# A decoder layer with product-key experts: three blocks of token tiles (2, 4, 2) in place of two (5, 3)

## The chip, the core and the metric

The kernel runs on one NeuronCore of a Trainium2 chip. The metric is the device time of one launch in microseconds. Before the change the median of three runs is 3268.28 us (3263.65 to 3278.97). TensorE multiplies matrices, VectorE and ScalarE work on rows of 128 partitions, GpSimd does row work too and issues the indirect transfers (gathers); SyncE issues most other transfers. Each engine runs its own list of instructions in order and waits at semaphores.

## The reference, cut to what matters

The layer has 1024 tokens of 1024 columns, in float32. Cut to its steps:

```
mod = silu(c) @ ada_w + ada_b                     # six vectors: sh1, sc1, g1, sh2, sc2, g2
h   = rms_norm(x) * (1 + sc1) + sh1
proj = h @ w_in                                   # latents of attention A, queries, keys, values of attention B
A: 4 heads, q and k/v from low-rank latents, rotary part of 64 columns, causal softmax
B: 4 heads, two softmax maps, (p1 - lambda * p2) @ v, norm of each head
x   = x + g1 * (concat(A, B) @ w_out)
h2  = rms_norm(x) * (1 + sc2) + sh2
q   = h2 @ w_q                                    # 8 heads, 2 halves of 128 columns
s   = q . sub_keys (128 keys for each half); top 16 of each half; top 16 of the 256 sums
g   = softmax of the 16 sums; e = their experts (first key * 128 + second key)
y   = sum over the 128 chosen experts of  g * gelu(u_tab[e] . h2) * v_tab[e]
out = x + g2 * y
```

`u_tab` and `v_tab` have 16384 rows of 1024 columns (64 MB each).

## The kernel before, in words

A tile is 128 tokens, so there are eight, 0 to 7. The products of the float32 operands are made in three passes over a high and a low part (`split`, `passes`, lines 272 to 286): weights come in raw, ScalarE writes the high part and VectorE or GpSimd the low part. The line numbers in profiles name these helpers often: 274 is the high part, 275 the low part, 284 to 286 the three passes.

The trunk has these stages. `project` (line 289) makes queries, keys and values of all eight tiles, with each weight loaded and split once, and puts them into DRAM. `block(t0, n)` (line 1200) then takes n tiles through `attend` (scores, softmax, values), `output` (output projection, residual, second norm) and `queries` (queries against keys, lists of the 16 best). It runs once for tiles 0 to 4 and once for tiles 5 to 7. In the second one the low parts of the weights are made on GpSimd, and `route_dense` (line 859) runs beside it: for each of the tiles 0 to 4 `routing` finds the chosen pairs on VectorE, and `matrix` makes, token by token, two one-hot rows A and B whose outer product on TensorE (line 897, tile `pg`) gives the token's weights over 128 x 128 experts. The rows B are made by GpSimd (line 886), by ScalarE or by VectorE after the letters of `SHARE`. The weights go to DRAM (`gd`).

The experts (line 1011) take tiles 0 to 4, 640 tokens, through all 16384 experts. Step j of 128 loads 128 rows of `u`, splits them, multiplies them with the tokens (`mm_u`, tile `mm`, line 1072), takes the Gelu, multiplies with the weights (`weigh`), splits the result, and adds products with rows of `v` four steps later (`mm_v`, tiles `pj` and `tp`, three passes; `add_y`).

Tiles 5 to 7 go another way beside it (`gathered`, line 929): for each of the 128 choices a gather brings the 128 chosen rows of `u` (512 KB, line 948 on GpSimd), and VectorE takes the dot product with the token (line 973). Then the same with rows of `v`: four gathers are one group, whose product with a window of coefficients goes to `y` on TensorE (line 993). The buffers of the gathers (`gath`, seven) turn in order; a gather waits for the one who read its buffer last. `PACE` says how far `gathered` is let on in each step of the experts.

The order of instructions in the trunk comes from a scheduler that follows the order of tracing and its own timeline; `weave` traces several streams in step by their costs. In the experts the order is the traced one (`manual_schedule`). PSUM has eight banks, which each stage takes by `banks`.

## Time and profile before

| | |
|---|---|
| median of 3 runs | 3268.28 us (3263.65 to 3278.97) |
| span of the profiled execution | 3271.8 us |
| TensorE busy | 3063.6 us, 94% |
| VectorE busy | 2180.9 us, 67% |
| ScalarE busy | 1199.3 us, 37% |
| GpSimd busy | 1288.8 us, 39% |
| read and written in HBM | 707.74 MB and 83.38 MB |
| mean granted TensorE clock | 0.974 |

The profiled execution's span is 3.5 us above the median and inside the range of the runs. Busy time is the time in which at least one instruction of the engine ran. In rows, PE is TensorE (PEld its weight loads), DVE VectorE, ACT ScalarE, POOL GpSimd, SP SyncE. A name such as `mm<-h2d,uh` says what is written and what is read. The stages of the trunk can be told by time: projections to 376 us, attention of tiles 0 to 4 to 505, their output to 584, their queries to 718, the second block and the matrices to 1189, and then the experts.

### The profile page before, as it was taken

What the parts mean: (1) busy time and instruction counts of PE and PEld (TensorE: products, weight loads), DVE (VectorE), ACT (ScalarE), POOL (GpSimd) and SP (SyncE); (2) the same over time, 40 slices, a digit from 0 to 9 for tenths busy, and PEclk for the clock granted to TensorE, in tenths of its full rate; (3) what the DMA queues carried; (4) which work ended last, traced back from release to release, by engine and by line L of the source; (5) the groups of instructions that cost most, each with busy time, mean ns of one, the idle gap of its engine ahead of it and who ended that gap; (6) DMA issues with size and microseconds to landing.
All of it is one profiled execution on the core that took longest, in us unless ns stands there. A gap on an engine that the chain in (4) does not pass through costs nothing.

```text
span 3271.8 us, 49470 instructions
## 1 busy us (share of the span) xinstructions
PE 3063.6 (94%) x17865; PEld 2569.6 (79%) x17865; DVE 2180.9 (67%) x5138; ACT 1199.3 (37%) x2372; POOL 1288.8 (39%) x1197
## 2 busy tenths in 40 slices
PE   6999989988887977999999999999999999999998
PEld 3678777977776967998888888888787888887776
DVE  4767366799898987888876666655665665633334
ACT  4644383337778862223222222222222222222221
POOL 1120000004799734334444444544454545523440
PEclk9999999989898999999999999999999999999999
DMA  8653637513357655778888888888888988878884
GB/s 268 200 167 113 206 99 240 182 36 120 116 178 238 182 155 198 267 257 285 300 281 295 289 296 302 305 317 312 310 306 316 322 323 318 310 271 292 285 295 158
DMA packets 375572, 794.38 MB, mean 243 GB/s; under 512 B 31392, under 2 KB 171040, under 8 KB 368672
## 3 DMA queue, kind: packets, MB, share of 16 engines
q0 software_dynamic: 114544, 418.46, 36.5%
q1 hardware_dynamic: 153200, 311.16, 28.1%
q10 hardware_dynamic: 107584, 61.61, 6.4%
q8 instruction: 140, 2.29, 0.3%
q14 instruction: 104, 0.85, 0.1%
HBM read 707.74 MB, written 83.38 MB: 242 GB/s over the span
## 4 chain that ended last, share of the span: by engine, by line
PE 66%; DVE 9%; DMA 8%; issue 6%; ACT 4%; POOL 3%; SPq 0%; POOLq 0%; ACTq 0%; DVEq 0%
PE mm L1072 20%; PE pj L284 6%; PE pj L285 6%; PE pj L286 6%; PE y L993 5%; PE tp L284 3%; PE tp L285 3%; PE tp L286 3%; PE pg L897 3%; DMA gath<-in_peer_v,eT 2%; DMA vr<-in_peer_v 2%; POOL gath L948 2%; DVE gath L973 1%; PE ov L655 1%; POOL B L886 1%
## 5 line engine op out<-in xcount | busy, mean ns | idle before, releaser
L1072 PE MATMUL mm<-h2d,uh 128*128 128x320 f32 x4096 | 774.3, 311 | 4.8 <-ACT C L1079 4.0
L948 POOL DMA_INDIRECT gath<-in_peer_u,ei x384 | 436.1, 1136 | 730.8 <-DVE gath L973 496.8
L1072 PEld LDWEIGHTS mm<-h2d,uh 128*128 128x128 f32 x4096 | 647.3, 189 | 44.6 <-issue 25.2
L948 POOL DMA_INDIRECT gath<-in_peer_v,eT x384 | 436.5, 1137 | 336.1 <-PE y L993 191.4
L973 DVE SCALAR_TENSOR_TENSOR gath<-gath,h 128x1024 f32<-128x1024 f32 x384 | 465.4, 1223 | 91.5 <-DMA gath<-in_peer_u,ei 73.6
L1072 PE MATMUL mm<-h2d,ul 128*128 128x320 f32 x2048 | 469.1, 310 | 20.3 <-POOL ul L275 13.3
L274 ACT ACTIVATE vh<-vr 128x512 fp32r<-128x512 f32 x256 | 160.6, 629 | 691.9 <-DMA vr<-in_peer_v 358.7
L886 POOL TENSOR_SCALAR B<-iota,T 128x128 f32<-128x128 f32 x240 | 264.1, 1108 | 269.7 <-DVE T L871 198.2
L275 DVE TENSOR_TENSOR vl<-vr,vh 128x512 fp32r<-128x512 f32 x248 | 169.8, 691 | 298.4 <-ACT vh L274 232.5
L1072 PEld LDWEIGHTS mm<-h2d,ul 128*128 128x128 f32 x2048 | 343.7, 189 | 22.0 <-POOL ul L275 13.7
L1079 ACT ACTIVATE C<-mm 128x640 f32<-128x640 f32 x128 | 89.6, 700 | 570.4 <-PE mm L1072 490.1
L1083 DVE TENSOR_TENSOR C<-C,G 128x640 f32<-128x640 f32 x128 | 105.2, 822 | 254.3 <-ACT C L1079 215.5
L285 PE MATMUL pj<-vl,CH 128*128 128x512 f32 x640 | 252.3, 394 | 11.1 <-POOL vl L275 9.5
L284 PE MATMUL tp<-vh,CH 128*128 128x512 f32 x640 | 255.4, 399 | 4.8 <-DVE cT L984 2.9
L285 PE MATMUL tp<-vl,CH 128*128 128x512 f32 x640 | 252.3, 394 | 3.1 <-DVE vl L275 2.3
L284 PE MATMUL pj<-vh,CH 128*128 128x512 f32 x640 | 254.6, 398 | 0.5 <-ACT vh L274 0.3
L286 PE MATMUL tp<-vh,CL 128*128 128x512 f32 x640 | 250.5, 391 | 0.0
L286 PE MATMUL pj<-vh,CL 128*128 128x512 f32 x640 | 250.4, 391 | 0.0
L897 PE MATMUL pg<-B,A 128*128 128x128 f32 x1280 | 197.0, 301 | 51.2 <-POOL B L886 21.9
L897 PEld LDWEIGHTS pg<-B,A 128*128 128x128 f32 x1280 | 177.4, 209 | 69.3 <-POOL B L886 35.5
L274 ACT ACTIVATE uh<-ur 128x512 fp32r<-128x512 f32 x256 | 157.9, 621 | 188.9 <-DMA ur<-in_u_t 166.7
L993 PE MATMUL y<-gath,zb 128*32 128x512 f32 x1536 | 202.4, 599 | 6.1 <-DMA gath<-in_peer_v,eT 6.0
(320 smaller groups left out, 5802.3 us busy)
## 6 DMA issues: line engine op xcount, KB each, us to landing
ur<-in_u_t SPq DMA_DIRECT2D x256, 256.0 KB
vr<-in_peer_v SPq DMA_DIRECT2D x256, 256.0 KB
gd<-gs ACTq DMA_DIRECT2D x20, 2048.0 KB
G<-gd SPq DMA_DIRECT2D x31, 1280.0 KB
adaw<-in_ada_w SPq DMA_DIRECT2D x32, 512.0 KB
wraw<-in_peer_w_q SPq DMA_DIRECT2D x128, 128.0 KB
wraw<-in_w_out SPq DMA_DIRECT2D x32, 256.0 KB
wraw<-in_w_in SPq DMA_DIRECT2D x24, 256.0 KB
```

The costliest lines, as they stand in the source:

```text
L274: nc.scalar.activation(hi, src, AF.Copy)
L275: (eng or nc.vector).tensor_sub(lo, src, hi.bitcast(FT))
L284: nc.tensor.matmul(out, ah, bh, start=start, stop=False)
L285: nc.tensor.matmul(out, ah, bl, start=False, stop=False)
L286: nc.tensor.matmul(out, al, bh, start=False, stop=stop)
L886: nc.gpsimd.tensor_scalar(B[:, m, :], iota128, T[:, 1, c + m:c + m + 1], T[:, 2, c + m:c + m + 1], op0=OP.is_equal, op1=OP.mult)
L897: nc.tensor.matmul(pg[:, o, :], A[:, o, :], B[:, o, :], start=True, stop=True)
L948: nc.gpsimd.indirect_dma_start(out=u, out_offset=None, in_=tab, in_offset=bass.IndirectOffsetOnAxis(ap=idx, axis=0))
L973: nc.vector.scalar_tensor_tensor(got[n], got[n], 1.0, q["h2"], op0=OP.mult, op1=OP.mult, accum_out=q["dots"][:, s:s + 1])
L993: nc.tensor.matmul(q["y"][RB * k:RB * k + RB, c, :], z[:, k, m % 2, RB - 1 - m:2 * RB - 1 - m], got[n + k][:, c * 512:(c + 1) * 512], star ...
L1072: nc.tensor.matmul(ps[:, o, 0:C2], s[:, k % 4, :], h2[:, mv, k, o * C2:(o + 1) * C2], start=st, stop=(k == 7 and s is l))
L1083: nc.vector.tensor_mul(c, c, gt[j // NJ][:, :, j % NJ, :])
```

## The change

The tiles are taken in three blocks: A is tiles 0 and 1, D tiles 2 to 5, B tiles 6 and 7. Block A goes through the whole trunk alone. Then the rest of the trunk (projections of D, block D, projections of B, block B beside `route_dense` for D) is woven with `gathered` for A, which is spread over 700 units of cost by `paced`. The experts take D, 512 tokens, and gather for B. So `project` runs three times and loads and splits its weights each time; `output` and `queries` run three times too, and GpSimd makes their low parts for D and B (`t0` is not 0). The gathers beside the trunk have five buffers (`NGA`), those beside the experts six (`NG`). `y` has its two PSUM banks for the whole run, so other stages have fewer: the projections four, the scores three or two, and `mm_u` now has two single banks (`mu`) in turn, for 512 columns each. The matrices are written for 16 tokens at a time and read by eight steps (`JG`), with two buffers. The shares of the one-hot rows are now half on GpSimd, with more on ScalarE and fewer on VectorE. Comments were taken out, which moves the line numbers: 886 is 882 now, 948 is 945, 973 is 970, 993 is 990, 1072 is 1060.

```diff
-DT = 5
-TOK = DT * P
+A0, AN = 0, 2
+D0, DN = 2, 4
+B0, BN = 6, 2
+TOK = DN * P
...
-GB = 32
+GB = 16
...
-SHARE = ['PAPDPAPD', 'PAPDPAPD', 'PAPDPAPD', 'PDADPDAD', 'DDADPDAD']
+SHARE = ['PAPAPAPD', 'PAPAPAPD', 'PAPAPAPD', 'PAPDPAPD']
...
+    ys = ctx.enter_context(tc.tile_pool(name="ys", bufs=1, space=PSUM, reuse_waits="tile"))
...
-            banks(c1, **(dict(mm=2, ov=1, pg=1) if t0 else dict(sc=4, ov=2)))
+            banks(c1, **(dict(sc=2, ov=1, pg=1) if t0 == B0 else dict(sc=3, ov=1)))
...
-            units = ([(kind, h, i, heads[kind, h]) for h in range(4) for kind in "md" for i in range(n)] if t0 else [(kind, h, i, heads[kind, h]) for h in range(4) for i in range(n) for kind in "md"])
+            units = [(kind, h, i, heads[kind, h]) for h in range(4) for kind in "md" for i in range(n)]
...
-    NG = 7
+    NG = 6
+    NGA = 5
-    def gathered(ts, w, rp, gath, zb):
+    def gathered(ts, w, rp, gath, zb, NG):
...
-            banks(c1, mm=1, ys=1, pj=2)
+            banks(c1, mu=2, pj=2)
...
-                        for o in range(2):
-                            nc.tensor.matmul(ps[:, o, 0:C2], s[:, k % 4, :], h2[:, mv, k, o * C2:(o + 1) * C2],
-                                             start=st, stop=(k == 7 and s is l))
+                        nc.tensor.matmul(ps, s[:, k % 4, :], h2[:, mv, k, :], start=st, stop=(k == 7 and s is l))
...
-            V = (((0, 0), (0, 1)), ((0, 2), (0, 3), (0, 4)), ((1, 0), (1, 1)), ((1, 2), (1, 3), (1, 4)))
+            V = (((0, 0), (0, 1)), ((0, 2), (0, 3)), ((1, 0), (1, 1)), ((1, 2), (1, 3)))
...
+    def projected(t0, n):
+        with ExitStack() as c1:
+            banks(c1, pj=4)
+            yield from project(t0, n)
+
+    def paced(g, total):
+        done = 0.0
+        for f in g:
+            yield (f - done) * total
+            done = f
...
-        run(weave((project(0, NT), 1.0), (ada_rest(), 0.2)))
+        run(weave((project(A0, AN), 1.0), (ada_rest(), 0.3)))
...
-        lists = pool(c1, "lists", DT)
-        run(block(0, DT))
-        run(weave((block(DT, NT - DT), 1.0), (route_dense(range(DT)), 2.6)))
+        gath = pool(c1, "gathA", NGA)
+        run(block(A0, AN))
+        def rest():
+            nonlocal lists
+            yield from projected(D0, DN)
+            lists = pool(c1, "lists", DN)
+            yield from block(D0, DN)
+            yield from projected(B0, BN)
+            yield from weave((block(B0, BN), 1.0), (route_dense(range(D0, D0 + DN), rp), 2.6))
+        run(weave((rest(), 1.0),
+                  (paced(gathered(list(range(A0, A0 + AN)), w, rp, gath, zb, NGA), 700.0), 1.0)))
     trunk.close()
-    experts()
+    experts(w, rp, zb)
```

GpSimd's order while the matrices are made, in the kernel before (B are one-hot rows, wl low parts of query weights; x is how many follow each other):

```order
L886 TENSOR_SCALAR B<-iota_98,T 128x128 x15
L275 TENSOR_TENSOR wl<-wraw,wh 128x256 x2
L886 TENSOR_SCALAR B<-iota_98,T 128x128
L275 TENSOR_TENSOR wl<-wraw,wh 128x256 x2
L886 TENSOR_SCALAR B<-iota_98,T 128x128 x3
L275 TENSOR_TENSOR wl<-wraw,wh 128x256 x2
```

The same place after the change, and GpSimd's way from there into the experts (gath are gathers, G the matrices, ul and vl low parts of the tables):

```order
L945 DMA gath<-in_peer_v,eT 128x1024 x4
L281 TENSOR_TENSOR wl<-wraw,wh 128x256 x2
L882 TENSOR_SCALAR B<-iota_101,T 128x128 x2
L281 TENSOR_TENSOR wl<-wraw,wh 128x256 x2
L882 TENSOR_SCALAR B<-iota_101,T 128x128 x4
L945 DMA gath<-in_peer_v,eT 128x1024 x4
L882 TENSOR_SCALAR B<-iota_101,T 128x128 x10
L945 DMA gath<-in_peer_v,eT 128x1024 x4
L882 TENSOR_SCALAR B<-iota_101,T 128x128 x12
L945 DMA gath<-in_peer_v,eT 128x1024 x59
L1053 DMA G<-gd 128x4096
L281 TENSOR_TENSOR ul<-ur,uh 128x512 x8
```

Gathers of block A now stand between the one-hots and the low parts, and 59 of the 512 stand behind the last one-hot, in front of all that GpSimd does for the experts.

TensorE's order at the same border, before (pg are the matrices, tp key scores, mm the first products of the experts):

```order
L897 MATMUL pg<-B,A 128x128 x8
L775 MATMUL tp<-keys,qh 128x128 x4
L1072 MATMUL mm<-h2d,uh 128x320 x4
L897 MATMUL pg<-B,A 128x128 x8
L775 MATMUL tp<-keys,qh 128x128 x2
L897 MATMUL pg<-B,A 128x128 x24
L1072 MATMUL mm<-h2d,ul 128x320 x2
L1072 MATMUL mm<-h2d,uh 128x320 x4
```

And after it (y are the products of gathered rows, eight to a group of four gathers, mu what mm was):

```order
L1060 MATMUL mu<-h2d,uh 128x512 x2
L893 MATMUL pg<-B,A 128x128 x16
L990 MATMUL y<-gath,zb_1554 32x512
L893 MATMUL pg<-B,A 128x128 x8
L990 MATMUL y<-gath,zb_1554 32x512
L893 MATMUL pg<-B,A 128x128 x4
L990 MATMUL y<-gath,zb_1554 32x512 x13
L990 MATMUL y<-gath,zb_1555 32x512 x16
L990 MATMUL y<-gath,zb_1554 32x512 x16
...
L990 MATMUL y<-gath,zb_1555 32x512 x16
L1060 MATMUL mu<-h2d,ul 128x512
```

After the last `pg` 125 rows of `y` follow each other (one row of 13 and seven of 16), and the experts come behind them.

## Rows read from the trace of the kernel before

**Rows 1.** Windows by stage, busy us: PE, PEld, DVE, ACT, POOL; clock; DMA:

```profile
0.00:45.00 45.00, 14.88 (x76) 3.37 (x76) 9.74 (x36) 9.16 (x17) 13.79 (x32) 0.97 0.91 300
45.00:376.00 331.00, 320.67 (x1656) 251.23 (x1657) 208.26 (x499) 165.56 (x407) 38.63 (x56) 0.98 0.53 165
376.00:505.00 129.00, 107.27 (x724) 91.50 (x723) 78.91 (x235) 92.80 (x248) 0.00 (x0) 0.93 0.54 154
505.00:584.00 79.00, 72.14 (x351) 60.24 (x349) 45.82 (x73) 24.75 (x52) 1.14 (x2) 0.94 0.80 290
584.00:718.00 134.00, 124.17 (x848) 122.51 (x849) 119.04 (x734) 45.30 (x109) 0.00 (x0) 0.95 0.27 82
718.00:882.00 164.00, 137.36 (x940) 120.60 (x940) 151.95 (x423) 119.65 (x232) 82.67 (x76) 0.94 0.42 126
882.00:1050.00 168.00, 134.06 (x767) 118.05 (x767) 144.01 (x330) 126.95 (x236) 154.61 (x135) 0.87 0.59 188
1050.00:1189.00 139.00, 130.77 (x910) 125.38 (x910) 134.84 (x514) 123.03 (x270) 98.46 (x110) 0.98 0.60 171
...
1262.00:3272.00 2010.00, 1975.12 (x11309) 1632.62 (x11307) 1233.55 (x2106) 464.50 (x759) 882.13 (x774) 0.99 0.83 292
```

**Rows 2.** Timeline of PE at the first experts: start, us, what, idle before:

```profile
1189.83 0.83 PE L1072 MATMUL mm<-h2d,uh 128*128 128x320 f32 x4
...
1216.46 0.90 PE L1072 MATMUL mm<-h2d,ul 128*128 128x320 f32 x2 [12.67 <-POOL ul L275]
```

**Rows 3.** Chain in order of time, in the experts: start, us, what:

```profile
1340.50 2.37 DVE gath L973 x4
...
1411.29 7.04 PE mm L1072 x48
1423.79 7.04 PE mm L1072 x48
```

**Rows 4.** Timeline of PE, second table's passes:

```profile
1409.99 0.39 PE L285 MATMUL pj<-vl,CH 128*128 128x512 f32 x1
1410.22 0.39 PE L286 MATMUL pj<-vh,CL 128*128 128x512 f32 x1
```

**Rows 5.** Groups by line: count, then busy us, mean ns, idle before:

```profile
L886 POOL TENSOR_SCALAR B<-iota,T 128x128 f32<-128x128 f32 x240 | 264.1, 1108 | 269.7 <-DVE T L871 198.2 <-PE pg L897 50.4 <-DVE nm L554 3.2
...
L993 PE MATMUL y<-gath,zb 128*32 128x512 f32 x1536 | 202.4, 599 | 6.1 <-DMA gath<-in_peer_v,eT 6.0
...
L275 POOL TENSOR_TENSOR wl<-wraw,wh 128x256 fp32r<-128x256 f32 (+1 forms) x80 | 74.4, 942 | 25.3 <-ACT wh L274 18.1 <-PE pg L897 3.2 <-PE tp L775 1.1
L275 DVE TENSOR_TENSOR wl<-wraw,wh 128x256 fp32r<-128x256 f32 (+3 forms) x120 | 63.2, 540 | 26.0 <-ACT wh L274 24.6 <-DMA wraw<-in_w_out 0.7 <-DMA wraw<-in_peer_w_q 0.5
```

**Rows 6.** Timeline of POOL, the first gathers:

```profile
1262.34 1.03 POOL L948 DMA_INDIRECT gath<-in_peer_u,ei  x1 [5.87 <-DVE ei L852]
1263.68 0.95 POOL L948 DMA_INDIRECT gath<-in_peer_u,ei  x1 [0.31 <-issue]
1264.93 0.94 POOL L948 DMA_INDIRECT gath<-in_peer_u,ei  x1 [0.30 <-issue]
...
1271.69 1.75 POOL L948 DMA_INDIRECT gath<-in_peer_u,ei  x1 [0.85 <-DVE gath L973]
```

**Rows 7.** Line 886: ns shortest, median, longest:

```profile
L886 POOL TENSOR_SCALAR B<-iota,T x240: 781/964/3799, 761.2 to 1199.1; 128x128 f32<-128x128 f32 x120
```

**Rows 8.** Timeline of PE, gathered rows of the last tile:

```profile
3171.45 1.92 PE L993 MATMUL y<-gath,zb 128*32 128x512 f32 x16
...
3177.97 1.90 PE L993 MATMUL y<-gath,zb 128*32 128x512 f32 x10 [0.67 <-DMA gath<-in_peer_v,eT]
```

**Rows 9.** Timeline of POOL, the gather between:

```profile
3173.63 0.94 POOL L948 DMA_INDIRECT gath<-in_peer_v,eT  x1 [6.21 <-PE y L993]
```

**Rows 10.** Timeline of DVE, the first dot products:

```profile
1270.19 1.22 DVE L973 SCALAR_TENSOR_TENSOR gath<-gath,h 128x1024 f32<-128x1024 f32 x1 [8.13 <-DMA gath<-in_peer_u,ei]
...
1276.84 2.29 DVE L973 SCALAR_TENSOR_TENSOR gath<-gath,h 128x1024 f32<-128x1024 f32 x1
```

More of the change, by code (lines that the diff above doesn't have):

```diff
@@ L316, in loadx @@
             def loadx(t):
-                xs[t] = wn.tile([P, D], FT, name="xt")
+                xs[t] = wn.tile([P, D], FT, name="xt", bufs=2 if t0 == A0 else 1)
                 nc.sync.dma_start(xs[t], xin[t])
@@ L565, in scores @@
             def scores(terms, L):
-                if t0:
-                    m = mmt()
-                    ps = [(m, 0, L)]
-                else:
-                    ps = [(bank("sc"), c, min(c + 512, L)) for c in range(0, L, 512)]
+                ps = [(bank("sc"), c, min(c + 512, L)) for c in range(0, L, 512)]
                 for b, c0, e0 in ps:
@@ L581, in turned @@
             def turned(w, L):
-                pT = pp.tile([P, nk, P], FT, name="pT", bufs=2 if t0 else 3)
+                pT = pp.tile([P, nk, P], FT, name="pT", bufs=2 if t0 == B0 else 3)
                 m = L // P
@@ L593, in load @@
                 hd = hdm if z == "m" else hdd
-                k = hd.tile([P, 2, nk * P], FR, name="hk" + z, bufs=1 if z == "d" and t0 else 2)
+                k = hd.tile([P, 2, nk * P], FR, name="hk" + z, bufs=1 if z == "d" and t0 == B0 else 2)
                 nc.sync.dma_start(k.bitcast(FT), kx[:, h, :, :nk * P])
@@ L1193, in experts @@
                     split_u(2 * j + 3)
[L1194 removed]
+                while tk[0] < 5:
                     step()
```

116 lines of the change are left out of this document (55 added, 61 removed).

## The prediction

> **What bounds the kernel now.** I read the windows cut at the stage borders first [rows 1], then the timelines inside the last stage, then the costs of what the change moves. The kernel has two halves. The trunk (projections, attention, output projection, queries, and the one-hot matrices of `route_dense`) runs until 1189.8 us, where the first matmul of the experts starts [rows 2]. The experts fill the other 2082 us. In the experts TensorE is the bound: it is busy for 1975 of the last 2010 us while VectorE has 1234 and GpSimd 882 [rows 1]. One step j of the experts starts a block of 48 matmuls of 320 columns that lasts 7.04 us, and the next block starts 12.5 us after it [rows 3]; between them stand 24 matmuls of 512 columns that follow each other every 0.23 us [rows 4], and 7.04 + 24 x 0.227 = 12.5, so nothing is idle there. The trunk is different. Between 718 and 1189 us VectorE is busy for 431 of 471 us (0.915), TensorE for 402, GpSimd for 336 [rows 1]: no engine has much room, and VectorE has least. Until 718 us GpSimd is nearly idle.
>
> **The change part by part, the experts.** Four tiles instead of five, two gathered tiles instead of three.
> - Keys times tokens: 24 matmuls of 512 columns for each j in place of 48 of 320, so 24 x 0.227 = 5.45 us in place of 7.04: 128 x 1.59 = 204 us less.
> - The other table: five tiles take 5 x 2 x 32 x 12 matmuls of 0.227 us = 872 us [rows 4]; a fifth goes, 174 us.
> - Gathered rows: 202.4 us for three tiles [rows 5], so 67 us less.
> - The start: now the first block begins at 1189.8 us and stands still for 12.67 us for a low part from GpSimd [rows 2]. In the new order the loads and splits for the first steps are in the queues during the end of the trunk; I take 15 us off (bounds 0 and 25).
> Other engines stay under TensorE here: VectorE loses a fifth of its three operations per step and a third of the dot products, GpSimd a third of its gathers. The transfers per us stay about level: by the code some 436 MB in place of 578 MB, in 1622 in place of 2082 us, 0.27 against 0.28 MB per us, while the windows show 292 GB/s now [rows 1]. So the experts take 2082 - 204 - 174 - 67 - 15 = 1622 us (bounds 1560 if the late waits go too, 1690 if six gather buffers in place of seven delay TensorE).
>
> **The trunk.** It loses the matrices of one tile and gets 512 gathers, 256 dot products, 64 groups of `y`, and the weights of the projections loaded and split three times instead of once. I cut it where the program order of GpSimd has its marks.
>
> *Until gather 134* (the last before the first split of block D on GpSimd). VectorE has the most to do. Projections now cost it 208 us for eight tiles [rows 1], of which the 50 weight splits are about 30 us (an estimate from the 0.54 us of one [rows 5]): 22.3 us a tile, so 134 us for six tiles and 60 us for two sets of splits. Attention cost 78.9 us [rows 1] for tiles 0 to 4, whose keys are 1 + 2 + 3 + 4 + 5 = 15 tiles long; tiles 0 to 5 have 21, so 110 us. Output of two tiles, 24 us (36 x 2/5 and 10 us of splits), queries 60 us (99 x 2/5 and 20 of splits). 134 dot products of 1.18 us (two take 2.37 us [rows 3]) are 158 us. Sum 546 us; at the share of 0.915 that the trunk has reached, 597 us, after 45 us of start [rows 1]: 642 us. Bounds: 590 (no idle VectorE at all) and 730 (share 0.8).
>
> *Gathers 135 to 275* (output and queries of D, projections of B). VectorE: 29 + 79 + 75 + 70 dots of 1.18 us = 266 us. GpSimd: 141 gathers, which follow each other every 1.25 us or more [rows 6], and 80 splits, 75 us [rows 5]: 251 us. TensorE from the same windows: 58 + 99 + 80 us and 17 groups of `y` of 2.1 us: 273 us. Three engines are full at once and wait for each other, each in its own order; TensorE's share between 376 and 1189 us is 0.80 to 0.94 [rows 1], so I take 0.88: 310 us (bounds 273 and 350).
>
> *Gathers 276 to 453* (block B and the matrices). GpSimd carries 178 gathers, 256 one-hot rows and 80 splits in one queue: 222 + 256 x 1.108 + 75 = 581 us with the mean of now, and 222 + 200 + 75 = 497 us with the shortest one-hot of 0.781 us [rows 5, 7]. VectorE is less full here than between 718 and 1189 us now, so I take a value between, 540 us, and 4% of waits: 560 us (bounds 497, and 720 below). What is queued behind a waiting gather is the next four one-hots and the low parts of the query weights, and TensorE waits for both.
>
> *The last 59 gathers.* They stand behind everything else on GpSimd, and on TensorE 125 rows of `y` (15.6 groups of eight) stand in front of the experts. There are five buffers, so a group's last row is asked for only after the group before it: `y` ended at 3173.37 us, the next gather started 0.26 us later, its rows were there 4.34 us after that [rows 8, 9]. With two more issues in between, a group takes 0.26 + 2.5 + 4.34 + 1.92 = 9.0 us, and 15.6 of them 141 us. TensorE works 2 of each 9 us. Bounds: 77 us if only the issue counts (62 x 1.25), 185 us at 11.9 us a group.
>
> Two hand-overs, where the coefficients are made and no gather is under way, cost about 10 us each (the first dot product came 7.85 us after its gather's issue [rows 6, 10]): 20 us. The trunk then ends at 642 + 310 + 560 + 141 + 20 = 1673 us, 483 us later than now, against 460 us saved in the experts. 1673 + 1622 = 3295, and with rounding 3300 us. The profiled execution has a span of 3271.8 us, 3.5 us above the median of the runs, so no correction is made: 3300 us is 1% slower. The point is that the work leaves a stage where GpSimd and VectorE had room and enters one where they had little.
>
> What each row on the shared side of GpSimd and VectorE shows: a gather's instruction took 1.03 us alone and 1.75 us beside VectorE's splits, a dot product 1.22 us and once 2.29 us [rows 6, 10]; one-hots run from 0.781 us to a mean of 1.108 [rows 5, 7]. The Trainium skill (SBUF — State Buffer, "Who interferes with whom") says that the pair of ports they share is an exclusive lock, held for a whole instruction. The trace agrees as far as it goes: the longer ones are longer by about one instruction of the other engine. By that rule the new trunk, in which both engines are full together, would pay more than the mean of now; that is the second rival.
>
> **The rivals.**
> 1. *The three parts of the trunk pack as well as GpSimd's sum allows, and it is faster.* For it: gathers are small pieces that fill holes, TensorE and GpSimd were idle for much of the time before 718 us [rows 1], and the dot products of the first part need no order against the projections. Each part then runs at its lower bound plus a little: 600 + 275 + 510 + 115 + 10 = 1510 us, and with 1622 us this gives 3130 us. Against it: 431 of 471 us is the best share that the trunk shows. It decides if the trunk ends before about 1630 us.
> 2. *GpSimd and VectorE shut each other out.* If one-hots take 1.3 us, gathers 1.64 us from start to start and splits 1.2 us, the third part is 292 + 333 + 96 = 721 us: 160 us more, 3460 us. For it: the 1.75 and 2.29 us rows. Against it: VectorE has fewer dot products in that part.
> 3. *TensorE is not the bound in the experts any more.* With six gather buffers the groups of the last tile come late, or transfers do: 70 us more, 3370 us. Against it: a group has 10.9 + 2 us for its four gathers there.
> That the gathers do not run beside the trunk at all is ruled out by the order: 453 of 512 stand before the last one-hot.
>
> **How the numbers follow.** My forecast, with the trunk ending between 1580 and 1780 us (3200 to 3400 us): 0.53. Rival 1: 0.24. Rival 2: 0.15. Rival 3: 0.08. A change of 0.5%, 16 us, is about what a measurement of this kernel can tell. Of the forecast's 0.53, 0.13 lies below 3252 us, 0.13 between 3252 and 3284, 0.27 above. So faster is 0.24 + 0.13 = 0.37, the same 0.13, slower 0.27 + 0.15 + 0.08 = 0.50. The range leaves out a tenth on each side: 3130 us, which is rival 1, to 3470 us, which is rival 2. The forecast's own range is 3200 to 3400 us.
>
> **What would show it.** The first matmul block of the experts that runs without a long gap starts near 1670 us. Before it stand about 140 us in which TensorE is busy for a fifth to a quarter and only `y` runs. Steps j start 10.9 us apart without `y`. In the third part GpSimd is busy for over 0.9 and VectorE under 0.8. GpSimd's one-hots have a mean between 0.8 and 1.1 us. The first dot product runs between 280 and 350 us. I would be wrong if the trunk ends before 1600 us (its parts overlap better than the fullest engine's share of now), if the gap before the experts is missing, or if the steps of the experts are longer than 12 us without `y`.

## The result and the profile after

The changed kernel takes 3733.65 us (median of four runs, 3719.09 to 3737.53) against 3270.99 us for the kernel before on the same chip: 1.140 times as long, 95% interval 1.137 to 1.143. The profiled execution is the fastest of the four, with a span of 3717.3 us.

Two times split this. The trunk ends, and the experts run without a gap, at 2078 us; before it was 1190 (where the first block began) [rows 2], and I had forecast 1673. The experts take 1639 us; before they took 2082, and I had forecast 1622. So the experts give back 442 of the 460 us that were reckoned, and the trunk takes 888 us more where 483 were reckoned. Of the error of 422 us 405 are in the trunk. (The marks differ a little: the first product that goes on without a gap, by which the new trunk is measured, comes at 1216 us in the kernel before [rows 2], so 26 of the 888 us belong to the mark.)

The windows of the changed kernel answer to [rows 1]. The columns are again PE, PEld, DVE, ACT, POOL busy, granted clock, DMA share and GB/s. The first gather is issued at 382 us and gather 134 at 701. GpSimd then stands still until the first low part of block D at 797. Gather 135 follows at 857, gather 276 at 1268 and gather 454 at 1909. The last row is the whole trunk:

```profile
0.00:382.00 382.00, 283.17 (x1519) 209.28 (x1519) 250.50 (x865) 185.25 (x449) 34.46 (x72) 0.88 0.66 209
382.00:701.00 319.00, 185.67 (x816) 148.02 (x816) 264.70 (x554) 93.98 (x218) 191.12 (x159) 0.72 0.93 318
701.00:797.00 96.00, 73.93 (x484) 63.44 (x483) 59.13 (x153) 57.74 (x147) 1.68 (x1) 0.88 0.22 69
797.00:1268.00 471.00, 372.82 (x1630) 239.07 (x1631) 324.73 (x1110) 158.74 (x359) 257.92 (x255) 0.88 0.79 276
1268.00:1909.00 641.00, 466.23 (x2431) 284.15 (x2426) 352.34 (x928) 334.32 (x700) 518.26 (x508) 0.87 0.75 245
1909.00:2066.00 157.00, 92.29 (x242) 15.03 (x238) 1.05 (x6) 0.00 (x0) 55.31 (x59) 0.72 0.62 207
2078.00:3717.00 1639.00, 1577.74 (x7170) 1185.18 (x7170) 1008.37 (x1750) 446.30 (x775) 579.75 (x527) 0.99 0.78 271
0.00:2078.00 2078.00, 1474.83 (x7111) 959.19 (x7112) 1254.90 (x3614) 830.03 (x1871) 1060.87 (x1055) 0.84 0.74 245
```

In the experts TensorE is busy for 1578 of 1639 us. In the trunk nothing comes near that. Until 797 us VectorE is busy for 574 us; without the first 45 us these are 565 of 752, or 0.75, where the prediction had 546 us of work at 0.915. From 797 to 1268 us TensorE is busy for 373 of 471 us, 0.79; the prediction had 273 at 0.88. From 1268 to 1909 us GpSimd is busy for 518 of 641 us, which is 0.81; the prediction had 540 of 560. TensorE's clock is 0.72 in two of the windows, and there it is the engine that waits. Over the whole trunk the granted clock is 0.84, where [rows 1] has 0.87 to 0.98.

The groups of the trunk between 100 and 2070 us answer to [rows 5] (count, then busy us and mean ns, idle time just before them and what ended it):

```profile
L990 PE MATMUL y<-gath,zb 128*32 128x512 f32 x1024 | 357.5, 721 | 195.9 <-DMA gath<-in_peer_v,eT 193.0 <-DVE gath L1000 2.0
L970 DVE SCALAR_TENSOR_TENSOR gath<-gath,h 128x1024 f32<-128x1024 f32 x256 | 317.5, 1246 | 136.7 <-DMA gath<-in_peer_u,ei 111.2 <-issue 25.0
L945 POOL DMA_INDIRECT gath<-in_peer_u,ei x256 | 304.5, 1190 | 285.4 <-PE y L990 107.8 <-DVE gath L970 87.9 <-issue 37.9
L945 POOL DMA_INDIRECT gath<-in_peer_v,eT x256 | 280.1, 1094 | 214.5 <-PE y L990 98.6 <-issue 50.2 <-DVE r_n L233 19.6
L882 POOL TENSOR_SCALAR B<-iota,T 128x128 f32<-128x128 f32 x256 | 259.0, 1018 | 16.1 <-PE pg L893 12.7 <-DVE T L867 1.9
```

The durations of GpSimd and VectorE are near those that the prediction used: a dot product takes 1.246 us (1.18 used), a one-hot row 1.018 us (1.108 used), a gather's instruction 1.09 to 1.19 us (1.25 from start to start used). The products `y` are not: TensorE is busy with them for 357.5 us, 5.6 us for each of the 64 groups, where 1.92 to 2.1 us were used. Between 797 and 1268 us they alone take 94.2 us, for some 18 groups:

```profile
L990 PE MATMUL y<-gath,zb 128*32 128x512 f32 x287 | 94.2, 679 | 52.9 <-DMA gath<-in_peer_v,eT 52.7
```

The waits on the right-hand side are large as well: TensorE stood for 196 us in front of `y`, mostly for gathers that had not landed, GpSimd for 285 and 215 us in front of gathers, mostly for a buffer that VectorE or TensorE had not read yet, VectorE for 137 us in front of dot products.

One standstill is visible by itself. GpSimd's timeline around it (start, us, what, idle before):

```profile
701.02 1.68 POOL L945 DMA_INDIRECT gath<-in_peer_u,ei  x1 [15.07 <-DVE gath L970]
797.28 1.29 POOL L281 TENSOR_TENSOR wl<-wraw,wh 128x512 fp32r<-128x512 f32 x1 [94.58 <-ACT wh L280]
799.46 4.06 POOL L281 TENSOR_TENSOR wl<-wraw,wh 128x512 fp32r<-128x512 f32 x3 [0.89 <-ACT wh L280]
...
856.68 1.76 POOL L945 DMA_INDIRECT gath<-in_peer_v,eT  x1 [19.56 <-DVE r_n L233]
```

For 94.6 us GpSimd waits for the high part of an output weight of block D, with 378 gathers behind it in its list. Block D's attention stands in front of that weight; its scores run on TensorE until 786 us. The next gather needs the row numbers for the second table, `eT`, which a transpose on TensorE makes. That transpose stands in TensorE's list behind the transposes of block D's output:

```profile
854.40 0.48 PE L963 MATMUL tp<-ident,ef 128*128 128x128 f32 x1 [0.91 <-DVE mL L281]
```

The tail came much as forecast. TensorE and GpSimd in it, where only `y` and its gathers are left, answer to [rows 8, 9]:

```profile
1996.91 1.60 PE L990 MATMUL y<-gath,zb 128*32 128x512 f32 x2 [2.85 <-DMA gath<-in_peer_v,eT]
1999.24 5.32 PE L990 MATMUL y<-gath,zb 128*32 128x512 f32 x14 [0.74 <-DMA gath<-in_peer_v,eT]
2007.74 1.91 PE L990 MATMUL y<-gath,zb 128*32 128x512 f32 x2 [3.18 <-DMA gath<-in_peer_v,eT]
...
2011.82 2.32 PE L990 MATMUL y<-gath,zb 128*32 128x512 f32 x12 [0.43 <-DMA gath<-in_peer_v,eT]
```

```profile
2003.47 0.94 POOL L945 DMA_INDIRECT gath<-in_peer_v,eT  x1 [6.09 <-PE y L990]
2004.71 0.94 POOL L945 DMA_INDIRECT gath<-in_peer_v,eT  x1 [0.30 <-PE y L990]
```

A group takes about 10.2 us (9.0 forecast; 1907.5 to 2065.9 us for the last 15.6 groups, about 158 us), and GpSimd stands for 6.09 us until `y` has read the buffer of the next gather. Fourteen rows of `y` take 5.32 us here at a granted clock of 0.54; twelve in the next group take 2.32 us at 1.00, and sixteen took 1.92 us in the experts before [rows 8]. The first rows of a group come in twos as its gathers land. In the whole window the clock is 0.72.

The border to the experts, and three steps of the experts from the chain of waits, answer to [rows 2, 3]:

```profile
2063.39 3.14 PE L990 MATMUL y<-gath,zb 128*32 128x512 f32 x11
2077.81 0.79 PE L1060 MATMUL mu<-h2d,ul 128*128 128x512 f32 x1 [11.28 <-POOL ul L281]
```

```profile
2228.49 5.69 PE mu L1060 x24
...
2239.62 5.44 PE mu L1060 x24
...
2250.50 5.45 PE mu L1060 x24
```

24 matmuls take 5.44 to 5.69 us and the next block starts 10.9 to 11.1 us after the one before; 5.45 and 10.9 were forecast.

### The profile page after: what moved, and what is told of

Same layout as the page of the kernel before. It is cut to its first block, busy times and chain, and to the rows that moved or that the text cites. A ratio compares the mean times of both kernels' runs of the same rounds, so it can differ in the third digit from the quotient of the medians.

```text
span 3717.3 us, 44072 instructions
## 1 busy us (share of the span) xinstructions
PE 3052.6 (82%) x14280; PEld 2144.4 (58%) x14280; DVE 2263.3 (61%) x5364; ACT 1276.3 (34%) x2646; POOL 1640.6 (44%) x1581
## 5 line engine op out<-in xcount | busy, mean ns | idle before, releaser
L945 POOL DMA_INDIRECT gath<-in_peer_u,ei x512 | 592.9, 1158 | 934.1 <-DVE gath L970 624.3
L945 POOL DMA_INDIRECT gath<-in_peer_v,eT x512 | 551.3, 1077 | 537.2 <-PE y L990 330.1
L970 DVE SCALAR_TENSOR_TENSOR gath<-gath,h 128x1024 f32<-128x1024 f32 x512 | 627.8, 1232 | 189.8 <-DMA gath<-in_peer_u,ei 151.6
L990 PE MATMUL y<-gath,zb 128*32 128x512 f32 x2048 | 490.8, 660 | 200.9 <-DMA gath<-in_peer_v,eT 198.0
L1060 PE MATMUL mu<-h2d,uh 128*128 128x512 f32 x2048 | 640.4, 394 | 3.5 <-ACT uh L280 3.5
L1060 PEld LDWEIGHTS mu<-h2d,uh 128*128 128x128 f32 x2048 | 386.1, 190 | 104.4 <-issue 17.6
L1060 PE MATMUL mu<-h2d,ul 128*128 128x512 f32 x1024 | 403.9, 394 | 21.7 <-POOL ul L281 12.5
L990 PEld LDWEIGHTS y<-gath,zb 128*32 128x32 f32 x2048 | 83.8, 114 | 453.1 <-DMA gath<-in_peer_v,eT 308.8
L280 ACT ACTIVATE wh<-wraw 128x256 fp32r<-128x256 f32 (+3 forms) x360 | 173.5, 496 | 231.0 <-DMA wraw<-in_w_in 94.7
L1060 PEld LDWEIGHTS mu<-h2d,ul 128*128 128x128 f32 x1024 | 194.2, 190 | 68.6 <-POOL ul L281 14.3
L291 PE MATMUL pj<-vl,CH 128*128 128x512 f32 x512 | 205.6, 402 | 10.9 <-DVE vl L281 10.2
## 6 DMA issues: line engine op xcount, KB each, us to landing
gd<-gs ACTq DMA_DIRECT2D x32, 1024.0 KB, 10.9
```

Source lines behind the costliest of these rows:

```text
L280: nc.scalar.activation(hi, src, AF.Copy)
L291: nc.tensor.matmul(out, ah, bl, start=False, stop=False)
L945: nc.gpsimd.indirect_dma_start(out=u, out_offset=None, in_=tab, in_offset=bass.IndirectOffsetOnAxis(ap=idx, axis=0))
L970: nc.vector.scalar_tensor_tensor(got[n], got[n], 1.0, q["h2"], op0=OP.mult, op1=OP.mult, accum_out=q["dots"][:, s:s + 1])
L990: nc.tensor.matmul(q["y"][RB * k:RB * k + RB, c, :], z[:, k, m % 2, RB - 1 - m:2 * RB - 1 - m], got[n + k][:, c * 512:(c + 1) * 512], star ...
L1060: nc.tensor.matmul(ps, s[:, k % 4, :], h2[:, mv, k, :], start=st, stop=(k == 7 and s is l))
```

## The experiments

The measure is the end of the trunk, which is the start of the first block of the experts on TensorE that goes on without a gap (2078 us in the changed kernel). The time behind it is 1639 to 1661 us in every kernel that has the changed kernel's experts, so differences in the trunk under some 15 us are not read. Kernels that were timed in several runs have an interval; the others, which leave out work that the result needs, have one run. In e2, e8, e14 and e15 the five buffers are five fixed tiles that are cleared once, in place of a pool's. The theories: A, waits in the chain of gathers (A1 their landing through five buffers, A2 what stands in front of them in queues); B, busy time; C, the three blocks by themselves; D, TensorE stopped by each group.

**e1. No gathers.**

```diff
-        run(weave((rest(), 1.0),
-                  (paced(gathered(list(range(A0, A0 + AN)), w, rp, gath, zb, NGA), 700.0), 1.0)))
+        run(rest())
+        for t in range(A0, A0 + AN):
+            nc.sync.dma_start(out.rearrange("(t p) d -> t p d", p=P)[t], x1d[t])
```

> Leaves out everything that is gathered for tiles 0 and 1 (their routing, 512 gathers, dot products, coefficients, products y); their output rows are a copy of the residual. What is left of the trunk is what the three blocks cost by themselves. Theory A (the chain of gathers is coupled to the rest by five buffers and three queues that are worked off in order, and this waiting makes the trunk long): the rest alone ends at 1130 to 1250 us (470 + 270 + 380 by the sums of the prediction without gathers), against 2078 us with them, so the gathers cost 830 us or more, for which VectorE has only 315 us of work. Theory C (three blocks with weights loaded three times, fewer PSUM banks and a small block A alone are slow, gathers or not): it ends at 1550 us or later. Experts as in the changed kernel, 1639 us, by both.

Measured: trunk end 1416 us, 3067.57 us in all. Between the two theories. The gathers cost 662 us; the rest is 296 us over the terms of the prediction without gathers, which are 470 + 270 + 380 = 1120 us (rounded up to 1130 in expectations). Windows, cut where TensorE changes stage (projections of A from 45, block A from 170, projections of D from 330, attention of D from 490, its output and queries from 630, projections of B from 800, block B and the matrices from 925):

```profile
0.00:45.00 45.00, 13.03 (x76) 3.14 (x76) 9.30 (x38) 11.12 (x20) 13.26 (x34) 1.00 0.89 288
45.00:170.00 125.00, 108.76 (x500) 64.97 (x500) 67.33 (x153) 56.66 (x129) 15.54 (x28) 0.91 0.88 282
170.00:330.00 160.00, 124.25 (x777) 110.12 (x776) 117.91 (x461) 89.89 (x234) 5.03 (x8) 0.82 0.53 169
330.00:490.00 160.00, 140.83 (x743) 121.07 (x741) 106.05 (x259) 85.68 (x210) 17.04 (x28) 0.96 0.59 180
490.00:630.00 140.00, 115.02 (x733) 97.08 (x733) 77.33 (x203) 82.92 (x217) 2.41 (x2) 0.89 0.32 99
630.00:800.00 170.00, 158.45 (x734) 128.06 (x732) 103.81 (x535) 64.41 (x147) 66.95 (x81) 0.96 0.45 153
800.00:925.00 125.00, 84.84 (x380) 70.41 (x380) 108.89 (x355) 61.66 (x140) 12.24 (x24) 0.78 0.43 129
925.00:1416.00 491.00, 344.66 (x2147) 297.91 (x2148) 297.73 (x868) 353.12 (x765) 336.15 (x339) 0.85 0.52 157
```

Until 630 us VectorE is busy for 378 us. The prediction's work for this part, without the dot products, was 546 - 158 = 388 us: right to 3%. But VectorE is not the fullest engine here. Behind the first 45 us it is busy for 0.63 of the time, and TensorE, which the prediction did not count in this part, for 489 of 585 us, 0.84. From 630 to 925 TensorE has 243 us (237 forecast) at 0.82 (0.88 forecast). From 925 GpSimd has 336 us (the prediction's 284 for one-hots and 75 for low parts are 359, at 0.96 some 380) at 0.68, and ScalarE with 353 us and TensorE with 345 are a little fuller. The work of the engines that were counted was right; which engine is the fullest, and its share, were not.

**e2. Rows of an eighth.** The table is read as rows of 128 columns, so the gathered rows all lie in its first eighth.

```diff
-                nc.gpsimd.indirect_dma_start(out=u, out_offset=None, in_=tab,
+                nc.gpsimd.indirect_dma_start(out=u[:, 0:P] if A else u, out_offset=None, in_=tab.rearrange("e (a b) -> (e a) b", b=P) if A else tab,
```

> Gathers for tiles 0 and 1 bring 128 of the 1024 columns (64 KB in place of 512 KB) into the same five buffers; dot products and products y run over all 1024 columns as before, so every instruction stays and only the bytes of these gathers fall to an eighth. Theory A1 (the time from issue to landing of a gather, with five buffers, is what the chain of gathers is made of): the landing falls from about 6 us or more under load to 2 or 3 us, a group of four goes from 10.6 to about 7 us in the tail, and the trunk ends 250 us earlier or more, below 1830 us. Theory A2 (gathers wait for other things in front of them in the queues of GpSimd and TensorE, whatever their size): the trunk ends 0 to 100 us earlier. Theory B (busy time of VectorE and GpSimd sets the trunk): 0 to 30 us earlier, since their work is the same.

Measured: trunk end 1927 us, 151 earlier. More than A2 and B allow, less than A1 wants: the landing is a part of the price, not the price. The run also settles a rival that the theories leave out: from 382 to 701 us the changed kernel's transfers are at a share of 0.93 and 318 GB/s, so they could bound this stretch. With rows of an eighth the same stretch is far from full, and the first low part of block D on GpSimd still comes at 802 us (797 in the changed kernel):

```profile
382.00:701.00 319.00, 177.73 (x768) 139.42 (x768) 273.88 (x580) 88.90 (x204) 189.74 (x162) 0.73 0.43 124
```

So the bytes do not bound the trunk until there; the 151 us are gained behind it.

**e3. Seven buffers.**

```diff
-    NGA = 5
+    NGA = 7
```

> Seven buffers in place of five for the gathers beside the trunk. Theory A1: three more gathers can be on their way while a group waits for its fourth, the tail goes from 10.6 to about 7 us a group, and the trunk ends 150 to 250 us earlier, the kernel near 3530 us. Theory A2: 0 to 80 us earlier, since the queues' order stays. Theory B: within 30 us of 3734 us.

Measured: trunk end 1937 us, 140 earlier; 3592.6 us, 1.096 (1.092 to 1.101) of the kernel before. Between A1 and A2 again, and about what small rows gave. GpSimd's standstill stays, from gather 134 at 629 to gather 135 at 798 us.

**e4. Low parts of block D on VectorE**, in `output` and in `queries`.

```diff
-                    split(w, h, l, nc.gpsimd if t0 else None)
+                    split(w, h, l, nc.gpsimd if t0 == B0 else None)
```

> The low parts of block D's output and query weights are made by VectorE in place of GpSimd, so they no longer stand in front of gathers on GpSimd. In the changed kernel no gather runs between 701 and 857 us: the next entry of GpSimd is such a low part, which waits for a weight that comes much later. Theory A2: gather 134 moves from 857 to about 720 us, the trunk ends 100 us earlier, the kernel near 3630 us. Theory A1: 0 to 40 us. Theory B: VectorE gets about 80 x 0.54 = 43 us more, so 0 to 40 us later.

Measured: trunk end 2071 us; 3719.09 us, 1.137 (1.133 to 1.141): no change. The low part is gone from GpSimd's list, and the standstill stays, now for the reason that stood behind it:

```profile
706.25 1.68 POOL L945 DMA_INDIRECT gath<-in_peer_u,ei  x1 [14.68 <-DVE gath L970]
853.09 1.68 POOL L945 DMA_INDIRECT gath<-in_peer_v,eT  x1 [145.16 <-DVE eT L965]
```

GpSimd waits 145 us for `eT`. The wait that the trace named had covered a second one, which ends at the same place.

**e5. Pace 450.**

```diff
-        ... w, rp, gath, zb, NGA), 700.0), 1.0)
+        ... w, rp, gath, zb, NGA), 450.0), 1.0)
```

> The gathers of tiles 0 and 1 are spread over 450 units of cost in place of 700. By the order of instructions 417 of 512 gathers (275 in the changed kernel) then stand before the first one-hot row on GpSimd and all 512 (453) before the last. Without any of these gathers the trunk ended at 1416 us, with them at 2078. Theory A2 (the place in the queues decides: too late in the order, so that the last 59 run alone and the transposes of the coefficients stand behind block D on TensorE): the tail of 169 us goes and gathers stand still for less than 60 us in place of 156 us near 700 us; the trunk ends near 1830 us, 250 us earlier, the kernel near 3480 us. Theory B (work): 2078 us within 40 us, because the same work is only done earlier. Theory D (each group of gathers stops TensorE, which works in order, for the same time wherever it stands): the tail's 169 us come back elsewhere, the trunk ends 0 to 80 us earlier.

Measured: trunk end 1990 us, 87 earlier; 3641.3 us, 1.113 (1.110 to 1.117). The standstill near 700 us is gone, since the transpose now comes at 673 us:

```profile
702.46 1.68 POOL L945 DMA_INDIRECT gath<-in_peer_u,ei  x1 [11.30 <-DVE gath L970]
704.44 1.99 POOL L945 DMA_INDIRECT gath<-in_peer_v,eT  x1 [0.30 <-issue]
706.73 1.51 POOL L945 DMA_INDIRECT gath<-in_peer_v,eT  x1 [0.30 <-issue]
```

The tail is gone too: the last `y` is at 1883 us, the last matrix at 1981. In the changed kernel these are 156 us without a gather and 158 us with nothing but `y`, and their removal gave 87: A2 falls, and it is nearest to D. The busy times are nearly the same (VectorE 1258 us, TensorE 1446 for 1475), so the rest came back as waits at other places; which ones was not followed up.

**e6. Short dot products**, for tiles 0 and 1.

```diff
-                nc.vector.scalar_tensor_tensor(got[n], got[n], 1.0, q["h2"], op0=OP.mult, op1=OP.mult,
+                m = 8 if t < A0 + AN else D
+                nc.vector.scalar_tensor_tensor(got[n][:, 0:m], got[n][:, 0:m], 1.0, q["h2"][:, 0:m], op0=OP.mult, op1=OP.mult,
```

> Dot products for tiles 0 and 1 run over 8 of the 1024 columns: VectorE loses about 256 x 1.15 = 295 us of work in the trunk, everything else stays. Theory B (VectorE's work): the trunk ends 200 us earlier or more. Theories A and D (waits in queues): 0 to 80 us earlier, mostly in the first 130 gathers, where dot products follow each other.

Measured: trunk end 1944 us, 134 earlier, for about 255 us of VectorE busy time less (1255 to 1000). Between B and A: half of the work shows. GpSimd's busy time falls too, from 1061 to 946 us, though its instructions are the same. Its gathers go from means of 1.190 (`u` rows) and 1.094 us (`v` rows) to 0.986 and 1.000, 76 us in all:

```profile
L945 POOL DMA_INDIRECT gath<-in_peer_u,ei x256 | 252.5, 986 | 364.1 <-DVE gath L971 235.9 <-PE y L991 58.7 <-issue 24.3
L945 POOL DMA_INDIRECT gath<-in_peer_v,eT x256 | 256.0, 1000 | 212.4 <-PE y L991 95.2 <-issue 43.2 <-DVE r_n L233 21.8
```

So gathers beside full-length dot products take longer, and the 134 us are not VectorE's work alone. The one-hot rows fall too, from 1.018 to 0.921 us, but e1, which has no dot products in the trunk, has 1.037; theirs cannot be put down to the dot products.

**e7. No y.**

```diff
-                for c in range(2):
+                for c in range(0 if t < A0 + AN else 2):
```

> Leaves out the products y for tiles 0 and 1 (TensorE's 1024 short matmuls of gathered rows); gathers of the second table still run into the five buffers, and nothing reads them. TensorE so waits for no gather of this table, and GpSimd waits for no y. Theory D: the trunk ends 250 us earlier or more, below 1830 us. Theory A1 (landing time of the gathers through five buffers): 100 us or less, since the gathers of a buffer still follow each other. Theory B: TensorE's own work in y (64 x 16 x 0.12 us = 123 us), so 60 to 120 us.

Measured: trunk end 1898 us, 180 earlier. Between D and B. Theory B had counted 123 us of `y`; TensorE's busy time falls by 241 us, from 1475 to 1233. The last product with `y` on VectorE is left out as well.

**e8. All three short.** The edits of e2 and e6, and in `y`:

```diff
+                e1 = 32 if t < A0 + AN else 512
...
-                        nc.tensor.matmul(q["y"][RB * k:RB * k + RB, c, :],
+                        nc.tensor.matmul(q["y"][RB * k:RB * k + RB, c, 0:e1],
...
-                                         got[n + k][:, c * 512:(c + 1) * 512], start=(m == 0), stop=(m == RB - 1),
+                                         got[n + k][:, c * 512:c * 512 + e1], start=(m == 0), stop=(m == RB - 1),
```

> For tiles 0 and 1 all three are short at once: gathers of 128 columns, dot products over 8, y over 32 of 512 columns in each matmul. What is left of the gathers' price is the issuing on GpSimd and waiting in the order of the queues. With rows alone short (e2) the trunk ended at 1927 us. Theory A2 or D: it still ends at 1780 us or later, since the waits stand in the same order. Theory B: work is gone, so it ends near the 1416 us of the kernel without gathers plus GpSimd's issuing, 1450 to 1550 us.

Measured: trunk end 1658 us, 420 earlier, between the theories once more. The single gains (151, 134 and, for `y` left out altogether, 180) come to 465, so they nearly add up. 242 us over the kernel without gathers stay.

**e9. More banks, without gathers.** The banks of `y` are taken for the experts only; the edits at five places are put together here.

```diff
-  banks(c1, pj=4) ... dict(sc=3, ov=1) ... dict(sc=2, ov=1, pg=1) ... dict(pj=3, pg=1)
+  banks(c1, pj=6) ... dict(sc=4, ov=2) ... dict(sc=4, ov=1, pg=1) ... dict(pj=5, pg=1)
```

> The kernel without gathers for tiles 0 and 1 (e1, trunk until 1416 us, where the sums of the prediction gave 1130) with the PSUM banks of the kernel before in the trunk: six in place of four for projections, output and queries, four and two in place of three and one for scores. The two banks of y are taken only for the experts. Theory E1 (fewer banks make the small blocks wait): the trunk ends at 1330 us or earlier. Theory E2 (weights loaded and split three times) and theory E3 (GpSimd's one-hot rows and low parts bound the last part): 1416 us within 25 us.

Measured: trunk end 1395 us, 20 earlier. E1 falls.

**e10. One projection, without gathers.**

```diff
-        run(weave((project(A0, AN), 1.0), (ada_rest(), 0.3)))
+        run(weave((project(0, NT), 1.0), (ada_rest(), 0.2)))
-            yield from projected(D0, DN)
-            yield from projected(B0, BN)
```

> The kernel without gathers for tiles 0 and 1 with the projections of all eight tiles made once in front of block A, as before the change; four banks as in e1. In e1 the three projections take about 125, 160 and 125 us, 410 together, and the one of the kernel before took 331. Theory E2: the trunk ends 80 us earlier, near 1335 us. Theories E1 and E3: 1416 us within 25 us.

Measured: trunk end 1347 us, 69 earlier, 2988.97 us in all, which is 79 less; the other 10 us are gained in the experts. E2 holds for these 69 of the 296 us.

**e11. Fewer one-hot rows on GpSimd, without gathers.**

```diff
-SHARE = ['PAPAPAPD', 'PAPAPAPD', 'PAPAPAPD', 'PAPDPAPD']
+SHARE = ['PAPDPAPD', 'PAPDPAPD', 'PDADPDAD', 'DDADPDAD']
```

> The kernel without gathers for tiles 0 and 1 with 11 of 32 one-hot rows on GpSimd in place of 16 (shares of the kind that the kernel before has), VectorE gets 8 of 32 more. In e1 GpSimd is busy for 264 of the 300 us from 1100 to 1400. Theory E3: 80 rows of 1.04 us go from GpSimd, the trunk ends 60 to 80 us earlier. Theories E1 and E2: 1416 us within 25 us.

Measured: trunk end 1441 us, 25 later. GpSimd's one-hot rows fall from 263 to 192 us, ScalarE loses 48 rows too, and VectorE's grow from 33 to 77 us. E3 falls: GpSimd is the fullest engine from 1100 to 1400 us, and taking work from it does not shorten the stage. The rows went to VectorE, which is busy there for 215 of 300 us, 192 in e1, so this run does not show what the stage would take if they cost nothing.

**e12. Four tiles through the experts, four gathered beside them, in the kernel before.** One part of the change alone; the list `V` and the banks of `queries` go by four tiles too.

```diff
-DT = 5
+DT = 4
-GB = 32
+GB = 16
```

> One part of the change alone: the kernel before, two blocks (0 to 3, 4 to 7), with four tiles through all experts in place of five and all four others gathered beside the experts; nothing is gathered in the trunk. One-hot matrices are written for 16 tokens at a time. Trunk near 1150 us by both theories. Theory T (TensorE bounds the experts): 2082 - 204 - 174 + 67 = 1771 us for the experts, 2930 us in all. Theory M (the transfers bound them): 436 MB and 256 MB more are 692 MB; at the 292 to 325 GB/s that the traces show in busy stretches this is 2130 to 2370 us, 3280 to 3520 us in all, and then the place for two of the four tiles can only be the trunk.

Measured: 3378.51 us, 1.0315 (1.028 to 1.035) of the kernel before. The trunk ends near 1179 us, and the experts take 2198 us: the time is that of theory M.

```profile
0.00:1200.00 1200.00, 1029.69 (x5771) 852.52 (x5772) 833.89 (x2688) 662.46 (x1452) 383.97 (x402) 0.93 0.55 160
1200.00:1300.00 100.00, 69.73 (x390) 61.09 (x390) 86.38 (x192) 21.45 (x36) 57.40 (x44) 0.80 0.67 232
1300.00:3376.00 2076.00, 1866.10 (x10811) 1352.34 (x10809) 1288.20 (x2285) 427.35 (x741) 1152.86 (x992) 0.97 0.92 334
```

334 GB/s at a DMA share of 0.92, where [rows 1] has 292 at 0.83; TensorE waits for the rest. The Trainium skill (DMA: Bandwidth & Descriptors, Specifications) gives about 358 GB/s as the HBM limit of one core, as half of what two cores share. The trace is near it; e3 has 343 GB/s from 381 to 629 us. That the transfers are the bound is argued from this share, since no run changes their bytes in this kernel. So all four gathered beside the experts cost time, and two beside the trunk cost more than they save.

**e13. Once, seven buffers, pace.** The projection of e10, and:

```diff
-    NGA = 5
+    NGA = 7
-        ... w, rp, gath, zb, NGA), 700.0), 1.0)
+        ... w, rp, gath, zb, NGA), 350.0), 1.0)
```

> All that gave time back and leaves the result whole, together: projections of all tiles once in front (78 us in e10), seven buffers (140 us in e3), gathers spread over 350 units in place of 700, so that 511 of 512 stand before the last one-hot (87 us in e5). If the gains add up (each removes another wait), the trunk ends at 2078 - 78 - 140 - 87 = 1773 us and the kernel takes about 3430 us, still slower than before. If seven buffers and the pace remove the same wait, the tail, the trunk ends near 1860 us and the kernel takes about 3515 us. Theory W, that enough slack brings the gathers down to the bounds of the prediction (1510 us), gives 3170 us and would beat the kernel before.

Measured: 3568.27 us, 1.091 (1.089 to 1.092); trunk end 1929 us, 149 earlier in place of the 305 expected. The gains do not add up. The whole projection now stands in front, and the gathers have only the time behind it, which may be why (no run isolates it):

```profile
0.00:590.00 590.00, 492.42 (x2665) 391.49 (x2665) 376.45 (x1193) 271.05 (x685) 62.43 (x98) 0.92 0.57 182
590.00:1930.00 1340.00, 953.05 (x4450) 568.33 (x4449) 841.69 (x2322) 491.74 (x1080) 969.00 (x925) 0.84 0.83 284
```

Until 590 us DMA is at a share of 0.57, then at 0.83 for 1340 us. This is the fastest of the whole versions that have gathers beside the trunk, and it is slower than the kernel before.

**e14. All short, pace 450.** The edits of e8 and of e5.

> As e8 (gathers of 128 columns, dot products over 8, y over 32), spread over 450 units in place of 700. e8's trunk ended at 1658 us, 242 us above the kernel without gathers. If these 242 us are the place in the order (a tail, transposes behind block D), the trunk ends at 1560 us or earlier. If they are issuing and routing work that stands in the way wherever it is, it ends at 1620 to 1680 us.

Measured: trunk end 1596 us, 62 earlier than e8. Between the two; the larger part of the 242 us is not the place in the order.

**e15. All short, nothing issued.** The edits of e8, and:

```diff
-                nc.gpsimd.indirect_dma_start(out=u, out_offset=None, in_=tab,
+                if not A:
+                  nc.gpsimd.indirect_dma_start(out=u, out_offset=None, in_=tab,
```

> As e8, but the gathers for tiles 0 and 1 are left out: dot products over 8 and y over 32 columns read five buffers that hold zeros. Routing, transposes and every wait between VectorE and TensorE stay; GpSimd loses 512 issues, 1.1 us each, 563 us of work. If issuing on GpSimd and its place in that queue are the rest of the price, the trunk ends at 1416 to 1500 us; if routing and order on VectorE and TensorE are, at 1600 us or later.

Measured: trunk end 1462 us, 196 earlier than e8. The windows of the two trunks, e8 first:

```profile
0.00:1658.00 1658.00, 1225.42 (x7110) 986.19 (x7110) 1003.50 (x3614) 825.93 (x1871) 963.09 (x1059) 0.83 0.53 165
```

```profile
0.00:1462.00 1462.00, 1122.78 (x7111) 912.70 (x7112) 973.91 (x3614) 817.12 (x1871) 473.89 (x548) 0.88 0.52 165
```

GpSimd loses 489 us of work, and the trunk 196. It also loses the small rows' landing, which this run does not tell apart from the issuing. What is left over the kernel without gathers, 46 us, is routing, transposes, the short dot products and `y`, and the waits between VectorE and TensorE.

## Why the prediction was wrong

*The experts* were right: 1639 us for 1622, steps 10.9 to 11.1 us apart, the transfers no bound (271 GB/s). Rival 3 falls.

*The step that failed* is the share at which the fullest engine of each part of the trunk was taken to run: 0.915 until gather 134, 0.88 until 275, 0.96 until 453. Measured are 0.75 for VectorE until block D's attention is done (797 us), 0.79 for TensorE until 1268 us and 0.81 for GpSimd until 1909. The work behind the shares was right to some 4% in the first part (565 us for 546) and in the third (518 for 540). In the second it was not: TensorE had 373 us for 273, of which `y` is 94 for 36, since a group takes 5.2 us there and the 2.1 us came from the experts.

I took 0.915 from one stretch, 718 to 1189 us, because it is VectorE's fullest. The rows of the whole trunk were there: in [rows 1] VectorE's busy times add up to 893 of 1189 us, 0.75, and TensorE's to 1041, 0.88. In the new trunk TensorE runs at 0.71 and VectorE at 0.60. Without the gathers they run at 0.77 and 0.63.

The 405 us fall into two parts. The trunk without gathers ended at 1416 where its terms give 1120: 296 us, of which 160 lie ahead of 630 us (630 for 388 / 0.915 + 45 = 469), 25 behind it and 111 in block B with the matrices. In the first of these the prediction left out the engine that is fullest without gathers. By the same rows TensorE's work there is 320.67 x 6/8 + 107.27 x 21/15 + (72.14 + 124.17) x 2/5 = 469 us [rows 1], and e1 has 489. At the 0.88 that the prediction takes for TensorE one part later this would have been 45 + 533 = 578 us; so, by this estimate, some 109 of the 160 us are the engine left out and the rest is its share. The three sets of weights are 69 of the 296 us (e10) and the banks 20 (e9); the other 207 no run took apart. The gathers cost 662 where 553 were forecast: 109 us.

*The gathers' price* was told apart: 420 us go when rows, dot products and `y` are short (e8), 196 when nothing is issued either (e15), 46 stay. The pieces of work that were taken away show with a part of their length: 134 us for 255 of VectorE and 115 of GpSimd (e6), 180 for 241 of TensorE (e7), 196 for 489 of GpSimd (e15). That is neither theory B, by which one engine's work sets the time, nor A2, by which the place in a queue does. My reading is that the trunk is a net of lists that are worked off in order, in which no engine is full, and a longer piece on any of them delays part of what stands behind it on the others. It fits these runs, but no run follows one delay through the lists. That a wait which is taken away is replaced by another is shown by e4, where GpSimd's standstill stayed with another releaser, and by e5, where 156 us of standstill and 158 us of tail gave back 87.

*The parts.* Gather 134 was issued at 701 us, inside the bounds of 590 to 730. But GpSimd was ahead of the others there: the attention of block D, which the sum has in the first part, ended only at 797 us, and GpSimd stood still until then. The prediction has no such wait: the low parts of block D and the transpose of `ef` stand on GpSimd and TensorE ahead of gather 135, and it counts the places alone where one-hots and gathers mix. By the work the first part took 797 us for 642, over the upper bound. The second, until gather 276, took 471 for 310 (bound 350), with the first of block B's attention already in it. Gathers 276 to 453: 641 us for 560, inside the bounds. From 1909 us to the experts: 169 us for 141, the gap before the experts and the `y` alone in it as described. These are 155, 161, 81 and 28 us more, less the 20 us of the two hand-overs, which are inside the parts: 405 us. TensorE was busy in the tail for 0.59 and not for a fifth to a quarter: at the granted clock of 0.72 `y` itself is long. The prediction has no term for the clock; the 2.1 and 1.92 us of `y` are from rows at a clock of 0.99 to 1.00. What the clock costs in the rest of the trunk no run tells apart.

*Rivals.* Rival 1 (packs better) is the one that failed most. Rival 2 did not come true as priced: one-hots, gathers and dot products kept nearly the durations of the kernel before, 1.02, 1.09 to 1.19 and 1.25 us, where it had 1.3 us for one-hots and 1.64 from gather to gather. A price of this kind is there all the same, and e6 sizes it: beside short dot products GpSimd's 512 unchanged gathers take 76 us less. That agrees with the rule of the Trainium skill that stands beside it in the prediction (SBUF — State Buffer, "Who interferes with whom"). The kernel before, where gathers run beside dot products too, had this price in its means already. Of the shown signs, GpSimd over 0.9 in the third part came out at 0.81, VectorE under 0.8 at 0.55, and the first dot product at 387 us in place of 280 to 350.

## What to carry to other kernels

When work is moved into a stage to fill its holes, count the work of every engine in each part, not of the one that looks fullest. Take the share that the fullest engine has over the whole stage, not over its best stretch, and expect it to fall when more lists wait for each other; here TensorE's fell from 0.88 to 0.77 by cutting the blocks smaller, and to 0.71 with the gathers. Take the price of a moved piece from a place where it waits and runs as it will: `y` cost 5.6 us a group in the trunk and 2.1 in the experts. Ask of each moved transfer how its reader holds up the list that it stands in: a gather has a reader on TensorE or VectorE and an issuer on GpSimd, and all three stop other work. A run that leaves the moved work out altogether tells first how much of the time belongs to it, and one that shortens all its parts at once tells whether the parts are worth taking singly.

## What was not expected of the hardware

A standstill named after one semaphore can have a second reason behind it: 94.6 us for a weight's high part, and without that, 145 us for a transpose, with the next gather at 857 and 853 us. Rows of `y` took 5.32 us for fourteen in the tail, at a granted clock of 0.54 (nearly all at the lower of the two levels, 1.2 and 2.4 GHz), and 2.32 us for twelve one group later at 1.00; sixteen took 1.92 us in the experts before [rows 8]. TensorE waits again and again there, and its clock over the whole tail is 0.72. Gathers beside the tables' loads brought the transfers to 334 GB/s at a share of 0.92 for 2 ms, and TensorE's share in the experts fell from 0.98 [rows 1] to 0.90. GpSimd's gathers of `u` rows took 1.19 us on average beside full dot products and 0.99 beside short ones (e6).
